# Splitting the last store of a rotary-embedding score kernel: two heads of 116 rows in a transfer of their own

## The chip, the cores and the metric

One core of one Trainium2 chip. The metric is the device time in microseconds (us) of one execution; every version was run several times. The timed runs of one batch were taken on one chip, with runs of the kernel before in between; the four batches of experiments fell on four chips (1 to 4, 5 to 8, 9 and 10, 11 and 12).

## The reference, cut to what matters

```python
batch, seq, heads, dim = 16, 512, 16, 64       # q, k: float32
q_rot = rotate(q, cos, sin)                    # halves of dim, by position
k_rot = rotate(k, cos, sin)
scores = np.einsum('bshd,bthd->bsht', q_rot, k_rot)   # 16 x 512 x 16 x 512, float32
```

67 MB go in and 268 MB come out. The output is stored as (batch, row, head, column), so that one row's 16 heads are 32,768 contiguous bytes and one row of two heads is 4096.

## The kernel before

The 512 rows of a batch are cut into four tiles of 128 (`C = 4`), so there are 64 tiles. For each tile TensorE makes the scores of two heads at a time, ScalarE (ACT) copies them from PSUM, the memory that TensorE writes its results to, into a staging buffer of 4 MB, and SyncE (SP) stores the whole buffer in one transfer. There are three staging buffers: the copies of tile i cannot begin before the store of tile i-3 has landed on all its DMA engines.

```python
stage_pool = ctx.enter_context(tc.tile_pool(name="stage", bufs=3))
o_v = out.rearrange("b (p c) h t -> b c p h t", c=C)
...
def scores(i, p, st):                       # tile i, pair of heads p
    ps = ps_s_pool.tile([P, 2, S], fp32, tag="ps_s", name="ps")
    ...                                     # two matmuls into ps
    nc.scalar.copy(out=so, in_=si)          # ps -> st[:, 2p : 2p+2, :]
    if b == 0 and p % 2 == 1:
        ...                                 # the first batch is stored in quarters
    elif b > 0 and p == HP - 1:
        nc.sync.dma_start(o_v[b, i % C], st)    # 128 rows x 32,768 B
...
for i in range(C, NST):                     # NST = 64
    ...
    st = stage_pool.tile([P, H, S], fp32, tag="stage", name="st")
    for p in range(HP):
        scores(i, p, st)
        ...
```

## Time and profile before

| | before |
|---|---|
| time, median of the three runs known at prediction | 802.37 us (801.93 to 802.97) |
| profiled execution, span | 799.2 us |
| busy share of the DMA engines in the middle | 90% or more in every slice |
| last copy by ACT ends | 777.75 us |
| twelve of 16 DMA engines end their data | 790.5 to 790.7 us |
| the last DMA engine ends its data | 797.86 us |

The one DMA engine that ends far behind the others, here the last, is called the straggler below, and the time by which it ends after the median of the 16 is its lag. One thing helps in reading this profile: a row of digits for the DMA is a mean over 16 engines, and one engine that works alone adds 1/16, which over a long slice is a 0. It becomes visible when a short window is cut into 40 slices. The lines themselves stand in the prediction.

### The profile page before, as it was taken

The page shows a single profiled execution, that of the slowest core. Times are in us where ns is not written, and L with a number is a line of the kernel's source. Part 1 is how long each engine was busy: PE and PEld are TensorE (multiplying, and loading weights), DVE is VectorE, ACT ScalarE, POOL GpSimd, SP SyncE. Part 2 cuts the span into 40 slices and gives each one's busy share as a digit, 9 for nine tenths or more (in the row PEclk, how much of TensorE's full clock was granted, in tenths as well). Part 3 has the DMA queues.
Part 4 walks back from the last instruction along what each step waited for, and adds up shares of the span by engine and source line. Part 5 has one row for each costly group of instructions (what it writes and reads, how often), then busy time and mean ns, then how long its engine had stood idle before and what let it go on. Part 6 is the DMA issues. An engine that isn't in the chain of part 4 may idle for free.

```text
span 799.2 us, 7712 instructions
## 1 busy us (share of the span) xinstructions
PE 690.9 (86%) x3072; PEld 299.7 (37%) x3072; DVE 544.6 (68%) x516; ACT 561.8 (70%) x647; POOL 0.7 (0%) x6
## 2 busy tenths in 40 slices
PE   4989998997979789797897978979789897889970
PEld 2444443443434334343343433434334343334420
DVE  7999987676858568585684866848668586685300
ACT  3878886776848578585775856768567685667870
POOL 0000000000000000000000000000000000000000
PEclk9999999899989899898998989989899898998995
DMA  9999999999999999999999999999999999998995
GB/s 353 420 426 430 431 416 430 426 433 440 424 438 423 428 435 424 442 425 433 427 433 431 432 431 429 433 433 424 426 428 435 433 402 430 438 426 362 429 422 249
DMA packets 17700, 336.17 MB, mean 421 GB/s; under 512 B 1792, under 2 KB 3072, under 8 KB 4096
## 3 DMA queue, kind: packets, MB, share of 16 engines
q1 hardware_dynamic: 17376, 335.55, 98.4%
q8 instruction: 24, 0.39, 0.2%
q10 hardware_dynamic: 288, 0.13, 0.1%
q14 instruction: 12, 0.10, 0.0%
HBM read 67.24 MB, written 268.44 MB: 420 GB/s over the span
## 4 chain that ended last, share of the span: by engine, by line
DMA 50%; PE 37%; DVE 5%; ACT 4%; issue 1%; ACTq 0%; DVEq 0%
DMA out_dram<-st 49%; PE ps L155 28%; PE bank L127 9%; ACT st L162 4%; DVE part L106 2%; DVE early L111 1%; DVE k_sb L107 1%; DVE k_sb L111 1%; DVE early L107 1%; DMA early<-in_k_dram 1%; DVE kT_t L142 0%; DVE q_sb L107 0%; DVE q_sb L111 0%; ACTq L270 0%; DVE qT_t L142 0%
## 5 line engine op out<-in xcount | busy, mean ns | idle before, releaser
L162 ACT COPY st<-ps 128x1024 f32<-128x1024 f32 x512 | 495.3, 1018 | 202.8 <-DMA out_dram<-st 113.9
L155 PE MATMUL ps<-kT_t,qT_t 64*128 64x512 f32 x2048 | 548.6, 654 | 70.9 <-ACT st L162 70.9
L155 PEld LDWEIGHTS ps<-kT_t,qT_t 64*128 64x128 f32 x2048 | 185.4, 198 | 258.9 <-issue 138.9
L142 DVE COPY qT_t<-bank 128x512 f32<-128x512 f32 x118 | 81.6, 691 | 202.4 <-PE bank L127 202.4
L127 PEld LDWEIGHTS bank<-ident,q_sb 128*128 128x128 f32 x480 | 55.6, 152 | 104.5 <-issue 101.9
L127 PE MATMUL bank<-ident,q_sb 128*128 128x128 f32 x480 | 86.8, 309 | 0.9 <-PE ps L155 0.9
L127 PEld LDWEIGHTS bank<-ident,k_sb 128*128 128x128 f32 x480 | 50.5, 141 | 95.1 <-DVE k_sb L107 38.0
L127 PE MATMUL bank<-ident,k_sb 128*128 128x128 f32 x480 | 78.7, 287 | 1.6 <-DVE qT_t L142 1.2
L142 ACT COPY kT_t<-bank 128x512 f32<-128x512 f32 x122 | 72.4, 597 | 6.2 <-PE bank L127 6.2
L107 DVE TENSOR_TENSOR q_sb<-q_sb,cos_t 128x1024 f32<-128x1024 f32 x60 | 73.5, 1225 | 2.1
L111 DVE TENSOR_TENSOR k_sb<-k_sb,part 128x1024 f32<-128x1024 f32 x60 | 73.5, 1225 | 2.1
L107 DVE TENSOR_TENSOR k_sb<-k_sb,cos_t 128x1024 f32<-128x1024 f32 x60 | 73.5, 1225 | 2.0
L106 DVE TENSOR_TENSOR part<-q_sb,ss_t 128x1024 f32<-128x1024 f32 x60 | 73.5, 1225 | 2.0
L106 DVE TENSOR_TENSOR part<-k_sb,ss_t 128x1024 f32<-128x1024 f32 x60 | 73.0, 1216 | 0.1
L111 DVE TENSOR_TENSOR q_sb<-q_sb,part 128x1024 f32<-128x1024 f32 x60 | 72.9, 1216 | 0.0
L127 PE MATMUL bank<-ident,early 128*128 128x128 f32 x64 | 10.5, 316 | 12.2 <-DVE early L111 10.3
L127 PEld LDWEIGHTS bank<-ident,early 128*128 128x128 f32 x64 | 8.3, 161 | 17.6 <-issue 14.3
L106 DVE TENSOR_TENSOR part<-early,ss_t 128x1024 f32<-128x1024 f32 x8 | 9.8, 1223 | 5.7 <-ACT ss_t L187 5.5
L111 DVE TENSOR_TENSOR early<-early,part 128x512 f32<-128x512 f32 x16 | 10.3, 687 | 0.2
L107 DVE TENSOR_TENSOR early<-early,cos_t 128x1024 f32<-128x1024 f32 x8 | 9.8, 1224 | 0.3
L142 ACT COPY qT_t<-bank 128x512 f32<-128x512 f32 x10 | 5.6, 615 | 3.2 <-PE bank L127 3.2
L142 DVE COPY kT_t<-bank 128x512 f32<-128x512 f32 x6 | 4.1, 685 | 1.3 <-PE bank L127 1.3
(9 smaller groups left out, 2.8 us busy)
## 6 DMA issues: line engine op xcount, KB each, us to landing
out_dram<-st SPq DMA_DIRECT2D x60, 4096.0 KB, 25.0
k_sb<-in_k_dram SPq DMA_DIRECT2D x15, 2048.0 KB, 28.4
q_sb<-in_q_dram SPq DMA_DIRECT2D x15, 2048.0 KB, 27.5
out_dram<-st SPq DMA_DIRECT2D x16, 1024.0 KB, 13.0
early<-in_k_dram SPq DMA_DIRECT2D x1, 1536.0 KB, 9.1
early<-in_q_dram SPq DMA_DIRECT2D x1, 1536.0 KB, 12.3
early<-in_k_dram SPq DMA_DIRECT2D x1, 512.0 KB, 4.7
early<-in_q_dram SPq DMA_DIRECT2D x1, 512.0 KB, 5.4
```

Source lines behind the costliest of these rows:

```text
L106: nc.vector.tensor_tensor(pv, xs, ss, op=mult)
L107: nc.vector.tensor_tensor(xc, xc, cs, op=mult)
L111: nc.vector.tensor_tensor(y, y, z, op=add)
L127: nc.tensor.transpose(bank[:, x, :], src, ident)
L142: copy(out=dst, in_=src)
L155: nc.tensor.matmul(out=po, lhsT=lhs[64 * r : 64 * r + 64, :], rhs=rh, start=True, stop=True)
L162: nc.scalar.copy(out=so, in_=si)
```

## The change

The store of the last tile alone is split. Heads 0 to 13 of all 128 rows go first, as one transfer. Heads 14 and 15 follow in two transfers, rows 0 to 115 and rows 116 to 127. The intent is that the number of rows decides how many DMA engines a transfer uses: 128 rows take all 16, 116 rows only four. The bytes of the last two heads thus move from all engines to a few.

```diff
+    def store(i, st):
+        o = o_v[i // C, i % C]
+        if i < NST - 1:
+            nc.sync.dma_start(o, st)
+            return
+
+        h = H - 2
+        nc.sync.dma_start(o[:, :h], st[:, :h])
+        nc.sync.dma_start(o[:116, h:], st[:116, h:])
+        nc.sync.dma_start(o[116:, h:], st[116:, h:])
...
         elif b > 0 and p == HP - 1:
-            nc.sync.dma_start(o_v[b, i % C], st)
+            store(i, st)
```

## The prediction

> **What bounds the kernel now.** I read the page first (slices, DMA queues, chain), then the DMA view and the engine-by-stretch table for the last microseconds, then the chain of waits from 740 us on, then SyncE's own waits, and at the end the packet records and semaphore updates that the trace holds for the last store.
>
> The page, whole execution. The DMA row is the busy share of the 16 DMA engines in tenths, one digit for each of 40 slices of 20 us:
>
> ```profile
> span 799.2 us, 7712 instructions
> DMA  9999999999999999999999999999999999998995
> GB/s 353 420 426 430 431 416 430 426 433 440 424 438 423 428 435 424 442 425 433 427 433 431 432 431 429 433 433 424 426 428 435 433 402 430 438 426 362 429 422 249
> HBM read 67.24 MB, written 268.44 MB: 420 GB/s over the span
> DMA 50%; PE 37%; DVE 5%; ACT 4%; issue 1%; ACTq 0%; DVEq 0%
> out_dram<-st SPq DMA_DIRECT2D x60, 4096.0 KB, 25.0
> ```
>
> The reader should see a kernel that keeps its DMA engines at 90% or more in nearly every slice, with 80% of the bytes going out through 4 MB stores. Only the last slice falls to 5 tenths: the tail is where the engines stand idle. The same row in fine slices of 0.3 us, from 788 us to 800 us:
>
> ```profile
> DMA  9250925022202000200020002000200000000000
> q1 hardware_dynamic: 57, 1.31, 25.4%
> ```
>
> A packet is counted where it begins. The tall digits are most engines starting together; after about 791 us only isolated 2s remain, one every four slices (1.2 us): one engine alone, working off its own queue. The stretches in a table (the last three columns are the clock, the DMA share and GB/s):
>
> ```profile
> 781.40:790.50 9.10, 0.00 (x0) 0.00 (x0) 0.00 (x0) 0.00 (x0) 0.00 (x0) 0.50 0.94 407
> 791.00:792.30 1.30, 0.00 (x0) 0.00 (x0) 0.00 (x0) 0.00 (x0) 0.00 (x0) 0.50 0.12 50
> 792.30:797.90 5.60, 0.00 (x0) 0.00 (x0) 0.00 (x0) 0.00 (x0) 0.00 (x0) 0.50 0.05 23
> ```
>
> 407 GB/s while all work; then 23 GB/s for 5.6 us, which is four packets of 32,768 B started by one engine. The packet records say the same: twelve engines finish the last store's data at 790.5 to 790.7 us, the others at 791.06, 791.94, 792.38 and 797.86 us. The last landing is at 798.33 us, the span ends at 799.2 us.
>
> The straggler is not new at the end. The sixteen updates of each store's semaphore give the lag of its last engine behind the median: 2.6 us for the store issued at 74.6 us, 5.8 at 335, 10.4 at 632, and 7.2 to 7.4 us in each of the last five. The chain from 740 us and SyncE's waits show what it costs:
>
> ```profile
> 749.63 19.52 DMA out_dram<-st
> 769.15 0.02 issue
> 769.25 1.02 ACT st L162
> 770.31 3.57 PE ps L155 x8
> 773.91 2.92 ACT st L162 x3
> ```
>
> ```profile
> SPq L167 <- ACT st L162: 26.9, 3, 10.4
> SPq L270 <- DMA out_dram<-st: 20.0, 3, 9.7
> ```
>
> The copies into the last staging buffer begin at 769.25 us, when the store issued at 749.63 us has landed on its last engine (median engine 761.8, straggler 769.15). SyncE issues the last store at 777.8 us and then only waits: 20.0 us over three stores. The straggler still has the store before in hand then (it lands there at 788.66 us), so its last eight packets run from 788.2 to 797.86 us. The end of the kernel is one DMA engine's queue, busy without a pause. The page's chain ends with ACT, because DMA after the last computed result is not on it; SyncE's waits show it.
>
> **What the Trainium skill says.** "DMA: Bandwidth & Descriptors", section "Why a DMA increments its semaphore by 16 and not by 1": the slowest dimension decides on how many engines a transfer runs, the largest number up to 16 that divides it, and on this path these are the lowest-numbered ones. So 128 rows use 16 engines, 116 rows use 4 (0 to 3), 12 rows use 12 (0 to 11). Before agrees for 128 rows (eight data packets per engine and store); nothing in it shows 116 or 12. The same page, "Latency and other measured facts": engines 7 and 15 are usually slower than the others, and it offers its cause only as a guess. Before shows one clear straggler, but the trace does not number the engines, so whether it is one of these no view tells. The same page, "Two DMAs through the same engine are not ordered": descriptors of one queue start in order on an engine. The straggler agrees: the last two stores follow each other on it.
>
> **The change part by part.** All stores but the last are untouched, and the instruction order on PE, DVE and ACT is the same; SyncE has 68 rows instead of 65. Everything happens after 777.8 us.
>
> Packet time by size, medians of before's records: 1024 B 46 ns, 3072 B 121, 8192 B 309, 16384 B 611, 32768 B 1213. The slope between the last and the 8192 is (1213 - 309)/24576 = 0.0368 ns per byte, with 7.7 ns fixed; it gives 121 ns for 3072 B, as measured. So I estimate 1062 ns for 28,672 B (14 heads of one row) and 158 ns for 4096 B (two heads).
>
> 1. The large part: 128 rows of 28,672 B, eight packets on each engine: 8 x 1062 = 8.50 us instead of 8 x 1213 = 9.70. Every engine gives up 1.21 us.
> 2. The 116 rows: 29 packets of 4096 B on each of four engines: 29 x 158 = 4.58 us, on these four alone. The other twelve get nothing.
> 3. The 12 rows: one packet, 0.16 us, on each of twelve engines.
> 4. Two more issues on SyncE of 0.33 us each (the duration of a store's issue before). They start near 778.1 and 778.5 us, while every engine is still busy with the store before (to 780.8 us at the earliest). Hidden.
>
> Sum on a normal engine of the four: 790.5 - 1.21 + 4.58 + 0.16 = 794.0 us; with the 1.9 us lag of the third-slowest kind, 795.9. Sum on the straggler:
> - if it is one of 12 to 15: 797.86 - 1.21 = 796.65 us; span and time 1.21 us shorter, 802.37 - 1.21 = 801.2;
> - if one of 4 to 11: 1.21 - 0.16 = 1.05 us shorter, 801.3;
> - if one of 0 to 3: 1.21 - 4.74 = 3.53 us longer, 805.9.
>
> In the first two cases the four loaded engines, at 794.0 to 795.9 us, still end before 796.65, so the straggler remains the end. The bytes taken from it are an eighth of one store; even a perfect levelling of the tail (797.86 down to about 791) would be worth some 7 us, 0.9% of the time.
>
> **The rivals.**
> (a) The straggler is one of the four. For: nothing in before numbers it. Against: the skill's 7 and 15, and that the change puts extra work on the lowest engines, which makes sense only if they have room. 805.9 us.
> (b) The lag is made by the profiling and absent in timed runs. Then sixteen level engines end together and the four would add 4.74 - 1.21 = 3.5 us: 805.9 us. Against: without the straggler the timed runs would be several us shorter than the profiled one, but they are 801.93 to 802.97 and the profiled run 800.97.
> (c) Packets of 4096 B on four engines cost more than the line says. The loaded engines have 796.65 - 794.0 = 2.6 us of room, so a packet could cost 158 + 2600/30 = 245 ns before it shows. The 1024 and 3072 B packets lie on the line. Beyond that, each 30 ns a packet would add 0.9 us.
> (d) The split costs at the end: three semaphores instead of one to wait for, each some tenths of a microsecond. Against: they come in while the straggler is still writing. At most 0.5 us, 801.7.
> (e) The lag at the end depends on the run (10.4 us at 632 us, 7.4 at the end), so the gain drowns: the three timed runs before lie 1.04 us apart, as much as the gain.
>
> **Range and chances.** I give 62% to the straggler being one of 12 to 15 (801.2), 28% to 4 to 11 (801.3), 10% to (a) or (b) together (805.9). On the first two lies a spread of about 0.6 us from run to run, and (c) and (d) only push upwards. I say 801.2 us, with 800.3 to 802.6 holding it 8 times in 10. A change of 2% is 16 us. The whole tail with one straggler is 7.3 us long and the worst case here adds 3.5, so neither side is within reach but by some upset of the timing as a whole: 0.5% and 1%.
>
> **What would show it right or wrong.** In the profile after: the 4 MB stores fall from 60 to 59, with one issue of 3584 KB, one of 464 KB and one of 48 KB. The packets under 8 KB rise by 128. There should be 116 + 12 packets of 4096 B at about 158 ns, and 128 of 28,672 B at about 1062 ns. After most engines end their large part (near 789.3 us) four engines go on for 4.6 us at some 4 x 26 = 104 GB/s, and one engine ends last near 796.7 us. The span should be near 798.0 us, with ACT's last copy still ending near 777.8. If the 116 rows land last, four engines being busy to 800 us, (a) or (b) is right. If the 116 rows' packets run on more than four engines, the reading of how rows choose engines is wrong. If the time before 777.8 us differs by as much as the end does, the comparison says nothing of the change.

## The result

| | before | after |
|---|---|---|
| median of six runs | 802.22 us (800.86 to 802.97) | 800.82 us (800.07 to 801.23) |
| mean | 802.10 us | 800.70 us |
| ratio | | 0.9983 (0.997 to 0.9995) |
| span of the profiled execution | 799.2 us | 799.0 us |

A ratio is the mean time of one kernel's runs over that of the other's of the same rounds, so it is not quite the ratio of the medians. The change is faster by about 0.2%.

The page after the change, whole execution:

```profile
span 799.0 us, 7715 instructions
DMA  9999999999999999999999999999999999998995
out_dram<-st SPq DMA_DIRECT2D x59, 4096.0 KB, 23.9
out_dram<-st SPq DMA_DIRECT2D x1, 3584.0 KB, 20.4
```

The body is the same to the digit; 59 stores of 4 MB are left, and one of 3584 KB is new. The other two new transfers are in the DMA view from 755 to 800 us:

```profile
out_dram<-st SPq DMA_DIRECT2D x1, 464.0 KB
out_dram<-st SPq DMA_DIRECT2D x1, 48.0 KB
```

464 KB are 116 rows of 4096 B, 48 KB are 12. The DMA view from 788 to 800 us in slices of 0.3 us:

```profile
DMA  2465434124222422432230002002000000000000
GB/s 96 137 191 164 150 82 150 68 109 205 109 82 82 191 109 96 191 82 82 96 150 41 27 0 96 0 0 96 0 0 0 14 0 0 0 0 0 0 0 0
```

Before, a lone 2 stood in every fourth slice from 791 us on. Now the slices up to about 794 us are filled, at 68 to 205 GB/s, and the comb of one engine shows only after that: 96 GB/s in one slice is one packet of 28,672 B in 0.3 us. The last entry, 14 GB/s, is one packet of 4096 B. The table of engines by stretches (busy times, which are all zero, then clock, DMA share and GB/s):

```profile
790.00:793.00 3.00, 0.00 (x0) 0.00 (x0) 0.00 (x0) 0.00 (x0) 0.00 (x0) 0.50 0.30 115
793.00:796.40 3.40, 0.00 (x0) 0.00 (x0) 0.00 (x0) 0.00 (x0) 0.00 (x0) 0.50 0.18 70
796.40:797.90 1.50, 0.00 (x0) 0.00 (x0) 0.00 (x0) 0.00 (x0) 0.00 (x0) 0.50 0.01 3
```

A share of 0.30 is 4.8 engines: the four with the 116 rows and the straggler. In the packet records the 116 rows' data end on four engines at 793.9 to 794.6 us; the straggler ends at 797.63 us. SyncE's waits from 755 us and the chain from 740 us:

```profile
SPq L281 <- DMA out_dram<-st: 17.6, 1, 17.6
SPq L152 <- ACT st L173: 0.5, 1, 0.5
```

```profile
748.85 20.87 DMA out_dram<-st
769.82 1.02 ACT st L173
```

SyncE again ends on a wait for a store. The small wait at line 152 is new: the large part needs only the first seven copies of the tile and is issued one copy before the last, and the 116 rows wait for that last copy. It gains nothing, because the large part queues behind the store before it.

The span fell by only 0.17 us (799.16 to 798.99), although the timed runs fell by 1.4. The chain shows why one profile must not be compared with another by its span. The ACT copy that waits for the straggler begins at 769.82 us here and at 769.25 us in the profile before, so the last tile was already 0.57 us late when the changed code began. The straggler's last 32,768 B packet, the end of the store before, came at 788.76 us against 788.18. From that moment to the end of the span it is 10.22 us after the change and 10.98 us before. Below, this difference is called the tail; it counts from the straggler's own clock and leaves out what happened earlier.

### The profile page after: what moved, and what is told of

It reads as the page before. It is cut to its first block, busy times and chain, and to the rows that moved or that the text cites. A ratio compares the mean times of both kernels' runs of the same rounds, so it can differ in the third digit from the quotient of the medians.

```text
span 799.0 us, 7715 instructions
## 1 busy us (share of the span) xinstructions
PE 691.3 (87%) x3072; PEld 299.3 (37%) x3072; DVE 544.6 (68%) x516; ACT 561.2 (70%) x647; POOL 0.7 (0%) x6
## 4 chain that ended last, share of the span: by engine, by line
DMA 50%; PE 40%; ACT 4%; DVE 3%; issue 1%; ACTq 0%; SPq 0%; DVEq 0%
DMA out_dram<-st 47%; PE ps L166 30%; PE bank L127 10%; ACT st L173 4%; DMA q_sb<-in_q_dram 2%; DVE part L106 1%; DMA early<-in_k_dram 1%; DVE q_sb L107 0%; DVE k_sb L107 0%; DVE k_sb L111 0%; DVE q_sb L111 0%; DVE early L107 0%; DVE kT_t L142 0%; ACTq L281 0%; DVE early L111 0%
## 5 line engine op out<-in xcount | busy, mean ns | idle before, releaser
L111 DVE TENSOR_TENSOR early<-early,part 128x512 f32<-128x512 f32 x16 | 10.3, 687 | 0.2
```

Source lines behind the costliest of these rows:

```text
L111: nc.vector.tensor_tensor(y, y, z, op=add)
```

## The experiments

Theory A: the end of the kernel is the queue of one DMA engine, and what the change is worth is the bytes that it takes from that engine, as long as the engines that get them still end earlier. Rival B: the gain is noise between batches. Rival C: the gain comes of splitting the store, whichever engines take the parts. The other open point is which engine straggles. Where the experiments change anything, it is only the split of stores, and all results are correct. Each diff is against the change; from experiment 2 on the change is shown in the form that experiment 1 gives it, and only the lines that differ from that are printed.

**1. The change again.** Its transfers are unchanged; the loop over groups of rows that the later versions use is in place.

```diff
-        nc.sync.dma_start(o[:116, h:], st[:116, h:])
-        nc.sync.dma_start(o[116:, h:], st[116:, h:])
+        a = 0
+        for n in (116, 12):
+            nc.sync.dma_start(o[a : a + n, h:], st[a : a + n, h:])
+            a += n
```

> The change itself again (two heads: 116 rows, then 12), the same transfers, on this chip and beside the versions sent with it. Theory A (the straggling engine's queue is the end, and it is one of engines 4 to 11): 1.05 us faster than before, ratio 0.9987, and its profile shows the last engine with exactly one packet of 4096 B after its eight of 28,672 B. Rival B (the first result is noise of the order of 1 us between batches of runs): ratio within 0.9995 to 1.0005.

Measured: 801.28 us median of five (799.96 to 802.72), before 801.31 of nine, ratio 0.9997 (0.9984 to 1.001). The tail is 10.25 us, and the last engine has one packet of 4096 B after eight of 28,672 B, as in the first profile. The trace repeats to 0.02 us. The timed runs of this batch do not show the gain: their ratio lies in the band that I had given to rival B, while the packets are those of theory A.

**2. The split without the shift.** The last two heads of all rows go in one transfer of 16 engines.

```diff
-        for n in (116, 12):
+        for n in (128,):
```

> The last two heads of all 128 rows in one transfer of their own, on 16 engines: the split without the shift of bytes. Theory A: every engine keeps its bytes, the straggler's queue ends 8 x 8 ns = 0.06 us later, ratio 1.0000 (0.9995 to 1.0005). Rival C (the gain comes of the split itself, shorter rows or an earlier last semaphore): as fast as the change, ratio 0.9983 to 0.9987.

Measured: 801.8 us, ratio 1.0009 (0.9995 to 1.0023), tail 11.12 us. The last engine works off eight packets of 28,672 B at 1062 to 1071 ns and eight of 4096 B at 159. The tail is longer than before by 0.14 us, so the split alone brings nothing: rival C falls by the trace, and no gain shows in the timed runs.

**3. The same bytes on seven engines.** This was meant to free the straggler entirely.

```diff
-        for n in (116, 12):
+        for n in (119, 7, 2):
```

> Two heads as 119 rows (7 engines), 7 rows (7 engines) and 2 rows (2 engines): the straggler gets none if it is engine 7 or above. Theory A: 1.21 us faster than before (ratio 0.9985), the last engine has no packet of 4096 B; the seven loaded engines end near 790.5 - 1.2 + 19 x 0.159 = 792.3. If the straggler were one of 0 to 6 it would carry 18 or 19 such packets: 1.7 us slower than before.

Measured: 804.0 us (803.42 to 804.5), ratio 1.0033 (1.002 to 1.0045), tail 13.83 us. I had expected a gain, with the loss as the alternative, and the alternative came: the last engine carries 18 small packets after its large ones, 17 of the 119 rows and one of the seven. They can be counted in the DMA view from 788 to 804 us, in slices of 0.4 us, where one packet of 4096 B is 10 GB/s (after the last 72):

```profile
GB/s 31 102 195 123 184 133 123 123 51 41 72 0 0 72 0 72 0 0 72 0 0 72 0 0 0 10 20 31 20 20 20 31 31 0 0 0 0 0 0 0
```

The straggler is thus one of the first seven engines, and not one of the first two, which the two rows would have given a 19th. The loss is larger than my 1.7 us, 2.6 by the means (803.91 against 801.28). In the trace the straggler's eighth large packet took 1879 ns and one small one 321; they make up 1.0 us.

**4. The same bytes on eleven engines.**

```diff
-        for n in (116, 12):
+        for n in (121, 7):
```

> The same bytes as 121 rows (11 engines, 11 rows each) and 7 rows (7 engines). If the straggler is one of 7 to 10 it carries 11 packets of 4096 B: 11 x 0.159 - 1.21 = 0.54 us slower than before (ratio 1.0007), 1.75 us slower than the seven-engine version beside it. If it is engine 11: no packet, 1.21 us faster. Rival B or C: no difference between the seven- and the eleven-engine version.

Measured: 802.1 us, ratio 1.0011 (0.9998 to 1.0023), tail 11.85 us, 12 small packets on the last engine (11 and one of the seven rows), in the same view:

```profile
GB/s 184 174 236 174 215 266 123 82 0 0 72 0 0 72 0 72 0 0 72 0 0 31 20 31 20 20 0 0 0 0 0 0 0 0 0 0 0 0 0 0
```

It is 1.8 us faster than the seven-engine version of the same chip by the means (802.14 against 803.91). The order of the two is the reverse of what I had expected for a straggler among engines 7 to 10, and it is what the packets on the straggler demand: 12 of them against 18. Had the bytes only been noise, or had the split alone mattered, the two would be equal.

**5. The same bytes on five engines.**

```diff
-        for n in (116, 12):
+        for n in (125, 3):
```

> Runs so far put the straggler among engines 4 to 6: one small packet from the 12-row transfer, none from the 4-engine one, 18 from 119 and 7 rows on seven engines. Now two heads as 125 rows (5 engines, 25 rows each) and 3 rows (3 engines). If the straggler is engine 4: 25 small packets, 25 x 0.159 - 1.21 = 2.8 us slower than before. If it is 5 or 6: none, 1.21 us faster, the five loaded engines ending near 790.5 - 1.2 + 26 x 0.159 = 793.4. By the skill's 7 or 15, also faster; but that reading has already failed. Tail from the straggler's last 32,768 B packet to the end of the span: 13.8 us or 9.8 us (before 10.98).

Measured: 805.02 us (804.52 to 805.45), ratio 1.0039 (1.0025 to 1.0053), tail 14.67 us. The last engine carries 25 small packets; 0.96 us of the tail is the excess of its last large packet, which took 1635 ns, and of two small ones with 432 and 272. The DMA view from 788 to 804 us, in slices of 0.4 us:

```profile
GB/s 133 92 174 102 102 143 92 113 92 10 72 0 0 72 0 0 72 0 72 0 0 0 10 20 31 20 10 31 20 20 31 20 31 10 0 0 0 0 0 0
```

The reader sees four engines' and the straggler's data up to 792 us, then the comb of the straggler's large packets (72), then a row of 10 to 31: its 25 packets of 4096 B, one after the other, to 801.5 us. So the straggler is among the first five engines. The next experiment, on the same chip, has 124 rows on the first four engines, and none of its packets on the straggler. On this chip it is thus the fifth, engine 4, if the lowest-numbered engines are the ones used, as the prediction quotes the skill: no trace numbers the engines, and what the runs show is an engine that five-engine transfers use and four-engine ones don't. On the chip of experiments 1, 3 and 4 the bounds are wider: not one of the first four (experiment 1), but one of the first seven (experiment 3), so engine 4, 5 or 6. One engine 4 on both is the simplest reading; it was shown on one.

**6. Three heads on four engines only.** Rows (124, 4), heads 13 to 15.

```diff
-        h = H - 2
+        h = H - 3
...
-        for n in (116, 12):
+        for n in (124, 4):
```

> Three heads as 124 rows and 4 rows, both on the four lowest engines: the straggler carries nothing of them. Theory A: it gives up 8 x 3 x 2048 x 0.0368 = 1.81 us, tail 10.98 - 1.81 = 9.2 us; the four engines end at 790.5 - 1.8 + 32 x 0.234 = 796.2, near the straggler's 796.1, so the gain is 1.3 to 1.8 us, ratio 0.9978 to 0.9985. Rival B: ratio within 0.9995 to 1.0005.

Measured: 800.8 us median of six, ratio 0.9993 (0.9975 to 1.001), tail 9.18 us, as predicted from the packet times. No small packet is on the last engine. The DMA view in the same window as above:

```profile
GB/s 143 123 174 92 92 174 108 128 108 77 174 77 189 92 61 97 15 97 15 0 0 0 0 0 0 0 0 0 0 0 0 0 0 0 0 0 0 0 0 0
```

All ends by 796 us. The timed runs, however, lie from 799.09 to 803.21 us, and their interval does not exclude no gain.

**7. Six heads in place of two.** Rows (116, 12), one number changed.

```diff
-        h = H - 2
+        h = H - 6
```

> The change with six heads instead of two (116 and 12 rows), one number changed. Theory A: the straggler ends 3.6 - 0.46 = 3.2 us earlier, but the four engines get 30 packets of 12,288 B at 0.46 us: 790.5 - 3.6 + 13.8 = 800.7, so they end last and the time is 2.8 us longer than before, ratio 1.0035. Rival (moving more off the straggler is always a gain): 3.2 us faster.

Measured: 804.72 us, ratio 1.0036 (1.0021 to 1.0052), 2.9 us slower by the means (804.82 against 801.93), where 2.8 had been predicted. The straggler ends its large packets at 795.24 us, well ahead; the four engines end at 800.0 to 800.69 us. The DMA view, 788 to 804 us:

```profile
DMA  1232324232323333213223222212330000000000
GB/s 61 92 143 123 143 123 174 92 143 123 143 123 143 123 143 123 113 61 123 123 92 123 92 123 123 92 61 92 123 92 0 0 0 0 0 0 0 0 0 0
```

About 122 GB/s until 795.2 us and 105 from there run on to 800 us, and no comb of one engine follows. The end has gone over from the straggler to the engines that got the bytes. This bounds the idea: the bytes moved must fit into the straggler's lag.

**8. The kernel before, once more.**

> The kernel before once more, for a second profile of its tail. Theory A: one engine again 7 us behind the others in the last stores, and 10.9 to 11.1 us from that engine's last packet of the store before to the end of the span, whatever the span is. If the straggler's lag differs by over 1 us, or if there is none, the tail of one profile doesn't stand for others.

Measured: 803.99 us (state unknown, one run), span 802.2 us. The DMA view, 788 to 804 us:

```profile
DMA  3193093093031010010010010010010000000000
```

The comb is there again, three microseconds later. The lag of the last engine behind the median is 8.5 us in this profile where it was 7.4 in the first, and the tail is 10.98 us in both. The limit of 1 us that I had set for the lag is just passed: the span and the lag differ from execution to execution, the tail does not.

**9 and 12. The change, third and fourth batch.**

> The change a third time, for the size of its gain in timed runs. In two profiles its tail was 10.22 and 10.25 us against 10.98 in two of before, so theory A gives 0.75 us, ratio 0.9991; the first batch gave 0.9983, the second 0.9997. Pooled over three batches, 0.5 to 1.2 us. Rival B (no gain in timed runs): pooled mean within 0.3 us of before.

> The change beside it: tail 10.2 to 10.3 us, ratio 0.998 to 0.9998.

Measured: third batch 800.64 us against 801.58, ratio 0.9988 (0.9976 to 1.0), tail 10.26 us; fourth batch 801.77 against 801.87, ratio 0.999 (0.9977 to 1.0003), tail 10.23 us. The four batches' differences of means are -1.40, -0.21, -1.02 and -0.50 us (6, 5, 5 and 5 runs of the change); weighted by those runs, -0.81 us. The four tails of the change lie at 10.22 to 10.26 us, against 10.98 twice before: -0.72 to -0.76. From the spread of the runs in each batch I estimate a standard error of 0.2 us for this mean; only the first batch's interval excludes no gain clearly by itself. Rival B, no gain at all, does not fit the pooled mean (all four signs are the same) nor the trace.

**10. One head in four earlier stores too.** The idea was that the straggler's queue never runs dry, so that bytes taken from it anywhere count.

```diff
+        moved = {16: 1, 28: 1, 40: 1, 52: 1, NST - 1: 3}.get(i, 0)
-        if i < NST - 1:
+        if not moved:
...
-        h = H - 2
+        h = H - moved
...                        # rows (124, 4) in place of (116, 12)
```

> The last store with three heads on four engines (124 and 4 rows), and one head so in four earlier stores, each 12 apart. Estimate: the straggler's queue never runs dry, so each head taken from it counts wherever it is: 7 heads x 0.6 = 4.2 us, as long as the four engines, which get 2.4 us a head more than the rest, have room; they use up to 4 x 2.4 = 9.6 us of it before the last store, spread over 600 us. If engine 4 sets the pace throughout: 3 to 4.5 us faster than before, ratio 0.9945 to 0.996. If the lag is only what the waits for buffers let build up, and the tail alone counts: as with three heads in the last store alone, 1 to 2 us, ratio 0.9975 to 0.999.

Measured: 804.14 us (801.88 to 807.5), ratio 1.0032 (1.0013 to 1.0051). Neither of my two cases came; it is slower. The landings of the store issued at 756.2 us have not one but two engines far behind the median, 7.8 and 7.2 us, and a third at 4.1 (before, in the third last store: 7.4, then 2.0 and 1.5). After the last store's large packets the 32 small ones follow on the engine that ends last, at 801.6 us; with 124 and 4 rows on the four lowest engines, it is one of those four. One head in four earlier stores has thus made a second straggler, and the three heads of the last store met it. What my estimate called room was not there for every engine: in the stream between, the DMA engines are 90% busy or more on average. All four were given the same bytes, but two of them are only 2 us behind at the end, so a lag is partly made up, and not alike on each. The bytes taken from the straggler early did count for a while: in the store issued at 714.8 us the last engine is 7.9 us behind, where it was 10.3 before. At 756.2 us nothing of that is left (7.8, before 7.4). Which of the earlier stores cost how much was not tried.

**11. Three heads again, beside the change.**

> Three heads on the four lowest engines once more (124 and 4 rows), now beside the change on one chip. Its first profile had a tail of 9.18 us (before 10.98, change 10.22 to 10.26), but its timed runs lay 4 us apart, ratio 0.9993 (0.9975 to 1.001). Theory A: tail 9.1 to 9.3 us again as long as the straggler is 7 us or more behind, ratio 0.997 to 0.999, about 1 us faster than the change. If the lag at the end is what sets the spread, its runs lie wider apart than those of the change, with no clear gain over it.

Measured: 800.79 us median of six (799.74 to 803.76), ratio 0.9988 (0.9971 to 1.0004), beside the change's 0.999. This time the tail is 10.29 us: the straggler ends its data at 796.92 us, but the four engines end at 796.3, 796.5, 796.98 and 798.01 us and so set the end. With three heads the two ends are about level, and a lag of 1.5 us of one of the four behind the others decides. The runs lie 4.0 us apart, those of the change 1.9, as the second of my expectations had it. By the means it is 0.5 us faster than the change on this chip (801.27 against 801.76), within the spread. I do not claim a version better than the change.

## Why the prediction was right or wrong

The time, 801.2 us, and the range held: 800.82 us measured. That the time came so near is in part luck: the straggler was another engine than the one I had bet on, but that moves the sum by only 0.16 us, and the first batch's gain of 1.4 us was above what the trace accounts for. Point by point:

- **One engine's queue is the end of the kernel: right.** Experiments 3, 4 and 5 put 18, 12 and 25 small packets on that engine and cost 2.6, 0.9 and 3.1 us by the means; experiment 2 with eight of them cost 0.6 with an interval that includes none; the change with one gains. The order of the times is the order of the packets on that engine, on two chips.
- **How many rows use how many engines: right.** Of the semaphore updates of each small transfer, four follow its data for 116 rows, seven for 119, eleven for 121, five for 125.
- **Packet times: right.** 159 ns for 4096 B where 158 was estimated, 1065 ns median for 28,672 B where 1062 was.
- **Which engine straggles: the case that I gave 62% was wrong.** It is engine 4 on the chip of experiments 5 and 6, and one of 4 to 6 on that of 1, 3 and 4, by the numbering that the prediction quotes: the case of 28%. In the profiles of the change on other chips, too, the straggler carries the one small packet of that case. This is the step that failed: I leant on the skill's remark on engines 7 and 15, and my third experiment, built on the same reading, failed for it. The cost of the error is small here only because the straggler lies just outside of the four loaded engines. Five engines instead of four would have cost 3 us.
- **The size of the gain: right in sign, somewhat off.** For an engine of 4 to 11 the sum said 1.05 us. The tail gives 0.76 in the first profile. The straggler's eight packets were not all at 1062 ns: one took 1146 and the last 1189, 0.21 us together, and the end came 0.06 us later after its last packet than before. All four profiles of the change have two such packets (1146 to 1171 and 1185 to 1204 ns), the last large packet of experiments 3 and 5 took longer still (1879 and 1635), and the splits over 16 and 11 engines have none. What lengthens them was not found. The first batch's 1.4 us is more than the tail gives; pooled over four batches the timed gain is 0.81 us.
- **Rival (a), the straggler among the four, did not come; (b) is ruled out** by the timed runs of the change, which on level engines would have been 3.5 us slower and were faster, and of experiment 7, which by its own sum (800.7 us against 790.5) would have been 10 us slower and was 2.9. Experiments 3 and 5 do not decide it: on level engines they end at 792.3 and 793.4 us, 1.8 and 2.9 us later than before, not far from the 2.6 and 3.1 that were measured.
- **Rival (c), dear small packets, did not come:** the median is 159 ns, though single ones took up to 761. **Rival (d)** is at most the 0.06 us above. The two further issues took 0.70 and 1.19 us, not 0.33 each; they stayed hidden all the same, since the second ended at 780.3 us and the large part landed on its first engine only at 788.9.
- **Rival (e) was truer than I had made it.** The lag before the last store ranges from 7.4 to 8.8 us in the profiles of before and the change, and the span of one profile (799.0) missed the 798.0 that I had announced, because its last tile began 0.57 us late. The condition in the prediction, that a difference of that size before the change's place makes the spans silent, applied.
- **Two slips in the prediction's readings**, without effect on the sum: the 4 MB stores carry 75% of the bytes moved (60 of them, 252 of 336 MB), and 80% is the share of all stores; and the packets under 8 KB rose by 144, not 128, since the two more transfers bring 16 more semaphore writes of 4 B.

## What to carry to other kernels

When the last transfer is long, look at when each DMA engine ends it, not at the mean busy share: here twelve of 16 engines were idle for 7 us while one worked off its queue, and the time was that queue. Bytes can be moved off such an engine by the number of rows of a transfer, but first find out which engine it is, by transfers on five, seven and eleven engines and by counting the packets on the last one; a step from four to five engines turned a gain of about 0.8 us into a loss of 3. Move no more than fits into its lag, try it at the end first (the one trial earlier in the stream lost), and judge an effect below the spread of the runs by a stretch of the trace that begins where the change begins.

## What the Trainium skill lacked or had wrong

- "DMA: Bandwidth & Descriptors", section "Latency and other measured facts", names engines 7 and 15 as usually slower; its best guess at the cause is one that it calls specific to transfers of the GpSimd path, and the stores here are issued by SyncE. By the numbering in the next point it was engine 4 on one chip (25 packets of the 128 rows with 125 on five engines, none with 124 on four) and one of 4 to 6 on another (none of 116 on four, 18 with 119 on seven); in every profile of before and the change one engine ended its part of the last store, heads 0 to 13 in the change, 7 to 9 us after the twelve on time. It loses a little with each store: between the landings of the stores issued at 741.0 and 749.6 us in before it took 9.94 us, the median engine 9.74. What makes it slow was not found.
- The same page, section "Why a DMA increments its semaphore by 16 and not by 1": the rule for the number of engines held for 116, 119, 121, 124, 125 and 128 rows; which engines they are the traces do not tell. The page does not say what else it serves for: a transfer with few engines as a means to take bytes off a slow engine (tail 10.98 to 10.22 us), or to find it.
- The same page's table of rules for kernel authors has the use of all 16 engines as a goal. At the end of this kernel two heads on four engines (and a little on twelve) left a shorter tail than on 16: 10.25 against 11.12 us, with means of 801.07 and 801.84 us of five runs each on one chip, a difference within the spread of the runs.
- No page says what becomes of the lag of one engine within a saturated stream. Here one head moved in four earlier stores left a second engine 7.2 us behind, though two others with the same extra bytes were only 2 us behind; together with three heads in the last store this cost 2.6 us by the means (804.27 against 801.70).
